# Delta net: triangular inverses as 64×64 blocks, one below the other, in place of 128×128 systems

## The chip, the cores and the metric

The kernel runs on one core of a Trainium2 chip. The metric is the time of one execution on the device in microseconds (us). PE is the matrix engine and PEld its weight loads, DVE the vector engine, ACT the scalar engine, POOL GpSimd; SP issues most DMAs. An fp32 matmul of the program appears in the trace as two passes, each with a weight load of its own.

## The reference

The program is two blocks on 256 tokens: a hybrid mixer with a mixture of experts, and a second block of four layers (forgetting attention, gated linear attention, delta net, forgetting attention). The change is in the delta-net layer, which has 8 value heads and 4 chunks of 64 tokens:

```python
def gdn_mixer(xn, w_in, conv_w, a_log, dt_bias, o_gain, w_out):
    bsz, s, _ = xn.shape
    hq, hv, d, L = GDN_QK_HEADS, GDN_V_HEADS, GDN_HEAD_DIM, GDN_CHUNK
    ...
    qkv = jax.nn.silu(causal_conv(qkv, conv_w))
    ...
    decay = jnp.where(causal, jnp.exp(jnp.where(causal, diff, 0.0)), 0.0)
    kb = kc * bc[..., None]
    vb = vc * bc[..., None]
    tri = jnp.where(strict, jnp.einsum('bhnld,bhnmd->bhnlm', kb, kc) * decay, 0.0) + jnp.eye(L, dtype=f32)
    u = lax.linalg.triangular_solve(tri, vb, left_side=True, lower=True)
    w = lax.linalg.triangular_solve(tri, kb * jnp.exp(gc)[..., None], left_side=True, lower=True)
    ...
    def step(state, inp):
        uu, ww, qkk, qd, kd, dec = inp
        v_new = uu - jnp.einsum('bhld,bhdv->bhlv', ww, state)
        o = jnp.einsum('bhld,bhdv->bhlv', qd, state) + jnp.einsum('bhlm,bhmv->bhlv', qkk, v_new)
        state = state * dec[..., None, None] + jnp.einsum('bhld,bhlv->bhdv', kd, v_new)
        return state, o
    ...
    return (o * jax.nn.silu(z)) @ w_out
```

For each head and chunk a unit lower triangular system of size 64 (`tri`) is solved.

## The kernel before

`gdn` (L1445) first projects the layer's input, convolves q and k and builds, per head, `U`: the strictly triangular products with their decay, for two halves of 128 tokens. So there are 16 systems of 128×128 (8 heads × 2 halves), each with two triangular blocks of 64 on its diagonal; the part between the two blocks is handled later.

The inverses are built by doubling. `TV` holds T (the inverse) and V (its transpose), 16 matrices of 128×128 each. `first` (L1566) makes the inverses of the 2×2 blocks: an identity from POOL, one predicated copy on DVE (L1571), four transpositions on PE (L1563) and a copy on ACT (L1574). Then come five levels, in which blocks of 2, 4, 8, 16 and 32 are joined in pairs. The systems are worked on in four groups of four, and a level of one group is three steps:

- `lower` (L1586): four matmuls with U as weights (L1592) into one PSUM bank, a memset on POOL (L1597), and a multiplication on DVE with the mask `below` (L1598), which gives X.
- `update` (L1602): four matmuls of V and X (L1610) and an addition on DVE into T (L1611). On the last level it makes V directly.
- `flipped` (L1613): four transpositions of T (L1563) and a copy on ACT into V (L1616), not on the last level.

The loop at L1631 runs these steps staggered: `lower` of step i, `update` of step i−2, `flipped` of step i−3. Between them it places the convolutions of v (`v_dense`, whose DVE work are L346, L354 and L359), their turning (`v_turn`, L1628 and L1629) and the multiplications of the queries (L1522, L1523). The projections that feed the convolutions (L271) stand before the stage in the order of PE, in both kernels. Then `upper`, `across`, `lower_half` and `rest` (L1655 to L1684) apply the inverses to v half by half, `result` follows, and `project` multiplies with the output weights.

Each engine executes its instructions in the program's order; the tile framework places the waits, and its scheduler may move instructions of independent pieces against one another when the program is built. PSUM tiles come from two pools of four banks (`ps`, `pd`). The constants `below` and `above` are made in `second_consts` (L1035 to L1050) on POOL.

## Time and profile before

| | us |
|---|---|
| median of 3 runs (lowest, highest) | 1313.79 (1312.56, 1315.02) |
| the profiled execution | 1312.93 |
| span of its instructions | 1311.3 |
| PE busy | 1149.3 |
| DVE busy | 589.4 |
| ACT busy | 492.8 |
| POOL busy | 141.6 |

The span is the time from the first to the last instruction; the profiled execution is 1.6 us longer than its span. A busy share is an average over stages with different limits, so a stage is read by its own stretch: the length of the stretch, the busy time of every engine in it, and the clock granted to PE (1.00 is 2.4 GHz). Matmuls are pipelined: the time from one to the next is read from starts or from a chain (length over count), not from the duration of one.

### The profile page before, as it was taken

How to read it: one execution, taken by the hardware profiler on the slowest of the kernel's cores; microseconds unless marked ns; L12 is line 12 of the kernel's file. 1: busy time of each engine (PE TensorE's matmuls, PEld its weight loads, DVE VectorE, ACT ScalarE, POOL GpSimd, SP SyncE). 2: the span in 40 equal slices, each digit the busy share in tenths (PEclk: the TensorE clock that was granted, in tenths of full speed). 3: DMA queues.
4: the chain of work that ended last, by engine and by line, in shares of the span. 5: the costliest groups of instructions: out<-in, count | busy, mean ns of one | idle time of the engine just before them, and what ended most of it. 6: DMA issues, size and time to landing. Idle time of an engine off the chain costs nothing.

```text
span 1311.3 us, 19298 instructions
## 1 busy us (share of the span) xinstructions
PE 1149.3 (88%) x7578; PEld 856.7 (65%) x7579; DVE 589.4 (45%) x1128; ACT 492.8 (38%) x1002; POOL 141.6 (11%) x420
## 2 busy tenths in 40 slices
PE   5999999987577676776767899999999999999998
PEld 4998999641223131321314788989788989897887
DVE  3976676410111010110102555666457776665554
ACT  4554455110101010100003467657455552356763
POOL 2000632000000000000000233010002111002310
PEclk8999999998889899888989999999999999999999
DMA  7843647899989999999999455444325430165620
GB/s 224 284 131 115 194 164 264 286 420 420 411 351 417 418 420 420 418 418 418 419 420 326 140 153 160 146 156 160 131 97 161 129 98 1 26 156 172 162 96 33
DMA packets 128633, 312.74 MB, mean 238 GB/s; under 512 B 7751, under 2 KB 73034, under 8 KB 112794
## 3 DMA queue, kind: packets, MB, share of 16 engines
q1 hardware_dynamic: 128186, 311.26, 65.6%
q8 instruction: 61, 1.00, 0.3%
q0 software_dynamic: 352, 0.20, 0.1%
q14 instruction: 34, 0.28, 0.1%
HBM read 310.39 MB, written 1.05 MB: 237 GB/s over the span
## 4 chain that ended last, share of the span: by engine, by line
PE 44%; DMA 22%; ACT 2%; DVE 2%; issue 1%; POOL 1%; SPq 0%; DVEq 0%; ACTq 0%
PE pd L292 19%; DMA we<-in_w_up 10%; PE pd L271 8%; DMA we<-in_w_down 7%; DMA we<-in_w_gate 4%; PE pd L959 2%; PE ps L1610 1%; PE ps L1592 1%; PE pd L980 1%; DMA w<-in_fox_w_in 1%; DVE wl L242 1%; ACT wh L241 1%; PE ps L1563 1%; PE ps L1176 1%; PE ps L991 1%
## 5 line engine op out<-in xcount | busy, mean ns | idle before, releaser
L271 PE MATMUL pd<-x,wh 128*128 128x256 f32 x1744 | 326.0, 287 | 2.3 <-DVE x L155 1.2
L242 DVE TENSOR_TENSOR wl<-w,wh 128x1024 fp32r<-128x1024 f32 (+1 forms) x206 | 251.1, 1223 | 127.3 <-ACT wh L241 126.7
L241 ACT CAST wh<-w 128x1024 fp32r<-128x1024 f32 (+1 forms) x206 | 214.5, 1045 | 205.5 <-PE pd L271 104.5
L271 PEld LDWEIGHTS pd<-x,wh 128*128 128x128 f32 x1744 | 275.2, 193 | 5.3 <-DVE x L155 1.8
L292 PE MATMUL pd<-wh,x 128*128 128x512 f32 (+3 forms) x896 | 252.7, 371 | 10.2 <-ACT wh L241 4.3
L271 PE MATMUL pd<-x,wl 128*128 128x256 f32 x872 | 248.1, 286 | 0.8 <-DVE wl L242 0.8
L959 PE MATMUL pd<-we,xt 128*32 128x512 f32 x1012 | 173.4, 724 | 79.1 <-DMA we<-in_w_up 50.6
L292 PEld LDWEIGHTS pd<-wh,x 128*128 128x128 f32 x896 | 162.1, 193 | 38.0 <-ACT wh L241 5.7
L959 PEld LDWEIGHTS pd<-we,xt 128*32 128x32 f32 x1012 | 40.0, 127 | 205.0 <-issue 86.4
L271 PEld LDWEIGHTS pd<-x,wl 128*128 128x128 f32 x872 | 167.7, 193 | 1.6 <-DVE wl L242 1.3
L292 PE MATMUL pd<-wl,x 128*128 128x512 f32 (+3 forms) x448 | 160.3, 370 | 1.5 <-DVE wl L242 1.4
L980 PE MATMUL pd<-we,sq 128*32 128x512 f32 x512 | 100.3, 642 | 33.9 <-DMA we<-in_w_down 28.1
L292 PEld LDWEIGHTS pd<-wl,x 128*128 128x128 f32 x448 | 85.2, 192 | 15.7 <-DVE wl L242 2.8
L992 DVE TENSOR_TENSOR hT<-hT,ps 128x512 f32<-128x512 f32 x32 | 22.0, 687 | 156.9 <-PE ps L991 156.9
L980 PEld LDWEIGHTS pd<-we,sq 128*32 128x32 f32 x512 | 24.7, 114 | 102.4 <-DMA we<-in_w_down 50.9
L969 DVE SCALAR_TENSOR_TENSOR cv<-cv,pd 128x512 f32<-128x512 f32 x8 | 5.5, 688 | 127.1 <-PE pd L959 127.1
L98 POOL TENSOR_SCALAR rq_y<-rs_v 128x8 int32<-128x8 int32 (+2 forms) x24 | 6.3, 264 | 514.9 <-DVE rs_v L186 417.0
L974 ACT COPY sq<-ps 128x512 f32<-128x512 f32 x8 | 4.7, 585 | 145.5 <-PE ps L972 145.5
L986 ACT COPY ys<-pd 128x512 f32<-128x512 f32 x16 | 9.4, 585 | 128.4 <-PE pd L980 128.4
L301 DVE SCALAR_TENSOR_TENSOR cv<-th,pd 128x512 f32<-128x512 f32 x8 | 5.5, 686 | 97.4 <-ACT th L300 97.4
L1299 POOL MEMSET at<- 128x1024 f32 x1 | 1.0, 952 | 438.1 <-DMA we<-in_w_down 438.1
L300 ACT ACTIVATE th<-pd 128x512 f32<-128x512 f32 x8 | 4.8, 597 | 100.7 <-PE pd L959 100.7
(476 smaller groups left out, 1407.3 us busy)
## 6 DMA issues: line engine op xcount, KB each, us to landing
we<-in_w_down SPq DMA_DIRECT2D x45, 1024.0 KB, 12.5
we<-in_w_up SPq DMA_DIRECT2D x40, 1024.0 KB, 12.4
we<-in_w_gate SPq DMA_DIRECT2D x37, 1024.0 KB, 12.4
w<-in_fox_w_in SPq DMA_DIRECT2D x30, 1024.0 KB, 8.0
we<-in_w_up SPq DMA_DIRECT2D x48, 512.0 KB, 13.8
we<-in_w_gate SPq DMA_DIRECT2D x46, 512.0 KB, 15.2
w<-in_w_in SPq DMA_DIRECT2D x22, 1024.0 KB, 9.2
we<-in_w_down SPq DMA_DIRECT2D x38, 512.0 KB, 14.9
```

Of the source, the lines that this page charges most:

```text
L241: nc.scalar.copy(h, v[:, k:k + m])
L242: nc.vector.tensor_tensor(l, v[:, k:k + m], h, OP.subtract)
L271: nc.tensor.matmul(acc[:, c], w[k][:, cs], x[:, k, p], start=start and c == 0 and at == 0 and i == 0, stop=stop and at == KC - 1 and i == ...
L292: nc.tensor.matmul(acc[j], x[:, k, p, ts], w[k], start=k == order[0] and i == 0 and (n != T or j == 0), stop=k == order[-1] and i == 2, sk ...
L959: mm = nc.tensor.matmul(out[32 * j:32 * j + 32], xt[:, k, 32 * j:32 * j + 32], w[name, 4 * q + j, k // 4][k % 4], start=k == 0, stop=k == ...
L980: mm = nc.tensor.matmul(py[h][32 * j:32 * j + 32], at[:, f, 32 * j:32 * j + 32], w["w_down", 4 * q + j, f // 2][f % 2][:, 512 * h:512 * h ...
L991: nc.tensor.matmul(pt[:, i * T:(i + 1) * T], ys[c // 4][:, c % 4 * P:(c % 4 + 1) * P], gst, start=True, stop=True)
L992: nc.vector.tensor_tensor(hT[:, 2 * u:2 * u + 2], hT[:, 2 * u:2 * u + 2], pt.rearrange("p (i t) -> p i t", i=2), OP.add)
L1176: nc.tensor.transpose(pt[:, (2 * i + j) * P:(2 * i + j + 1) * P], n4[w, j][:, 2 * o + i], s.ident)
L1563: nc.tensor.transpose(pt[:, a * P:(a + 1) * P], x[:, a], s.ident)
L1592: nc.tensor.matmul(pt[:, a * P:(a + 1) * P], U[:, 2 * g4 + a // 2, (a % 2) * P:(a % 2 + 1) * P], t[:, a], start=True, stop=True)
L1610: nc.tensor.matmul(pt[:, a * P:(a + 1) * P], l[:, a], m[:, a], start=True, stop=True)
```

## The change

A system is now a 64×64 block. The two blocks of a half stand one below the other: block 0 in partitions 0 to 63, block 1 in partitions 64 to 127, so TV is [128, 2, 16, 64]. Each product is one matmul per block on a quarter of the PE array (rows and columns 0 to 63, or 64 to 127), with both blocks' results in the same PSUM bank on different partitions (`products`). There are two groups of eight in place of four groups of four. V is no longer a transposition of T: `update` forms two products, one for T and one for V, into one bank, and adds both on DVE; `flip`, `flipped` and the copies of L1616 are gone. `lower` and `update` move only the 32 columns that are used. The loop goes level by level: `lower` of both groups, a `v_dense`, `update` of both, a `v_turn`; the queries come in levels 2 and 3. The masks are remade per half with 14 small copies on POOL, `upper` works in two row halves, and `lower_half` reads the 64×64 block.

```diff
+    below = s.tmp.tile([P, 5, 32], F32, tag="kk", name="below", bufs=1)
+    nc.gpsimd.memset(below, 1.0)
...
+    s.below = s.const.tile([P, 5, 16], F32, name="below")
+    s.above = s.const.tile([P, 32], F32, name="above")
+    s.ident64 = s.const.tile([P, 64], F32, name="ident64")
+    for o in range(2):
+        rows = slice(64 * o, 64 * o + 64)
+        for i in range(5):
+            n = 16 >> i
+            nc.gpsimd.tensor_copy(s.below[rows, i, :n], below[rows, i, n * o:n * o + n])
+        nc.gpsimd.tensor_copy(s.above[rows], above[rows, 32 * o:32 * o + 32])
+        nc.gpsimd.tensor_copy(s.ident64[rows], s.ident[rows, rows])
...
-        return s.conv_silu(None, pq, rb2, lambda i, j: cw[:, 16 * j + 2 * u + i:16 * j + 2 * u + i + 1], after=made.get(2))
+        return s.conv_silu(None, pq, rb2, lambda i, j: cw[:, 16 * j + 2 * u + i:16 * j + 2 * u + i + 1], after=made.get(1))
...
-    TV = s.xp.tile([P, 2, 16, P], F32, tag="x", name="TV")
+    TV = s.xp.tile([P, 2, 16, 64], F32, tag="x", name="TV")
...
-    def flip(x):
-        pt = s.ps.tile([P, 512], F32, name="ps")
-        for a in range(4):
-            nc.tensor.transpose(pt[:, a * P:(a + 1) * P], x[:, a], s.ident)
-        return pt.rearrange("p (a t) -> p a t", a=4)
-
-    def first(g4):
-
-        t, v = sys4(Tm, g4), sys4(Vm, g4)
-        nc.gpsimd.tensor_copy(v, s.ident[:, None, :].to_broadcast([P, 4, P]))
-        odd = lambda x: x.rearrange("p o (n c) -> p o n c", c=2)[:, :, :, 1]
-        made[g4] = nc.vector.copy_predicated(odd(v.rearrange("p (o j) t -> p o (j t)", o=2)).rearrange("p o (j n) -> p o j n", j=2),
-                                  s.above.bitcast(I32)[:, None, None, :].to_broadcast([P, 2, 2, P // 2]),
-                                  odd(U[:, 2 * g4:2 * g4 + 2, :T]).rearrange("p o (j n) -> p o j n", j=2)).ins
-        nc.scalar.copy(t, flip(v))
...
+    both = [(slice(64 * o, 64 * o + 64), 64 * o) for o in range(2)]
+
+    def eight(t, g):
+        return t[:, 8 * g:8 * g + 8]
 
     def halves(x, lev):
 
         x = x.rearrange("p a (n c) -> p a n c", c=4 << lev)
         return x[:, :, :, :2 << lev], x[:, :, :, 2 << lev:]
 
-    def lower(i):
-
-        lev, g4 = divmod(i, 4)
-        t = sys4(Tm, g4)
-        pt = s.ps.tile([P, 512], F32, name="ps")
-        for a in range(4):
-            nc.tensor.matmul(pt[:, a * P:(a + 1) * P], U[:, 2 * g4 + a // 2, (a % 2) * P:(a % 2 + 1) * P], t[:, a],
-                             start=True, stop=True)
-        X[i] = s.tmp.tile([P, 4, P], F32, tag="kq"[i % 2], name="X")
-        xl, xr = halves(X[i], lev)
+    def products(out, l, m):
+
+        for a in range(8):
+            for rows, off in both:
+                nc.tensor.matmul(out[rows, a], l(a, rows, off), m(a, rows), start=True, stop=True)
+
+    def bank():
+        return s.ps.tile([P, 512], F32, name="ps")
+
+    def first(g):
+
+        t, v = eight(Tm, g), eight(Vm, g)
+        nc.gpsimd.tensor_copy(v, s.ident64[:, None, :].to_broadcast([P, 8, 64]))
+        for rows, off in both:
+            made[g] = nc.vector.copy_predicated(
+                v[rows].rearrange("p (o j) (n c) -> p o j n c", j=2, c=2)[:, :, :, :, 1],
+                s.above[rows].bitcast(I32)[:, None, None, :].to_broadcast([64, 4, 2, 32]),
+                U[rows, 4 * g:4 * g + 4, :T].rearrange("p o (j n c) -> p o j n c", j=2, c=2)[:, :, :, off // 2:off // 2 + 32, 1]).ins
+        pt = bank().rearrange("p (a t) -> p a t", a=8)
+        products(pt, lambda a, rows, off: v[rows, a], lambda a, rows: s.ident64[rows])
+        nc.scalar.copy(t, pt)
...
-    def lower(i):
-
-        lev, g4 = divmod(i, 4)
-        t = sys4(Tm, g4)
-        pt = s.ps.tile([P, 512], F32, name="ps")
-        for a in range(4):
-            nc.tensor.matmul(pt[:, a * P:(a + 1) * P], U[:, 2 * g4 + a // 2, (a % 2) * P:(a % 2 + 1) * P], t[:, a],
-                             start=True, stop=True)
-        X[i] = s.tmp.tile([P, 4, P], F32, tag="kq"[i % 2], name="X")
-        xl, xr = halves(X[i], lev)
+    def products(out, l, m):
+
+        for a in range(8):
+            for rows, off in both:
+                nc.tensor.matmul(out[rows, a], l(a, rows, off), m(a, rows), start=True, stop=True)
+
+    def bank():
+        return s.ps.tile([P, 512], F32, name="ps")
+
+    def first(g):
+
+        t, v = eight(Tm, g), eight(Vm, g)
+        nc.gpsimd.tensor_copy(v, s.ident64[:, None, :].to_broadcast([P, 8, 64]))
+        for rows, off in both:
+            made[g] = nc.vector.copy_predicated(
+                v[rows].rearrange("p (o j) (n c) -> p o j n c", j=2, c=2)[:, :, :, :, 1],
+                s.above[rows].bitcast(I32)[:, None, None, :].to_broadcast([64, 4, 2, 32]),
+                U[rows, 4 * g:4 * g + 4, :T].rearrange("p o (j n c) -> p o j n c", j=2, c=2)[:, :, :, off // 2:off // 2 + 32, 1]).ins
+        pt = bank().rearrange("p (a t) -> p a t", a=8)
+        products(pt, lambda a, rows, off: v[rows, a], lambda a, rows: s.ident64[rows])
+        nc.scalar.copy(t, pt)
+
+    for g in range(2):
+        first(g)
+
+    X, last = {}, [None]
+
+    def lower(lev, g):
+
+        nb = 16 >> lev
+        tl = halves(eight(Tm, g), lev)[0]
+        pt = bank()[:, :T].rearrange("p (a t) -> p a t", a=8)
+        products(pt, lambda a, rows, off: U[rows, 4 * g + a // 2, (a % 2) * P + off:(a % 2) * P + off + 64],
+                 lambda a, rows: tl[rows, a])
+        X[g] = s.tmp.tile([P, 8, 64], F32, tag="kq"[g], name="X")
+        xl, xr = halves(X[g], lev)
         nc.gpsimd.memset(xr, 0.0)
-        nb = P // (4 << lev)
-        last[0] = nc.vector.tensor_tensor(
-            xl, halves(pt.rearrange("p (a t) -> p a t", a=4), lev)[0],
-                                s.below[:, lev, :nb][:, None, :, None].to_broadcast([P, 4, nb, 2 << lev]), OP.mult).ins
-
-    def update(i):
-
-        lev, g4 = divmod(i, 4)
-        t, v, x = sys4(Tm, g4), sys4(Vm, g4), X[i]
-        l, m, out, side = (v, x, t, 0) if lev < 4 else (x, v, v, 1)
-        out = halves(out, lev)[side]
-        pt = s.ps.tile([P, 512], F32, name="ps")
-        for a in range(4):
-            nc.tensor.matmul(pt[:, a * P:(a + 1) * P], l[:, a], m[:, a], start=True, stop=True)
-        nc.vector.tensor_tensor(out, out, halves(pt.rearrange("p (a t) -> p a t", a=4), lev)[side], OP.add)
-
-    def flipped(i):
-        lev, g4 = divmod(i, 4)
-        if lev < 4:
-            nc.scalar.copy(halves(sys4(Vm, g4), lev)[1], halves(flip(sys4(Tm, g4)), lev)[1])
+        last[0] = nc.vector.tensor_tensor(xl, pt.rearrange("p a (n c) -> p a n c", n=nb),
+                                          s.below[:, lev, :nb][:, None, :, None].to_broadcast([P, 8, nb, 2 << lev]), OP.mult).ins
+
+    def update(lev, g):
+
+        nb = 16 >> lev
+        t, v, x = eight(Tm, g), eight(Vm, g), X[g]
+        pt = bank().rearrange("p (i a t) -> p i a t", i=2, a=8)
+        xl, vr = halves(x, lev)[0], halves(v, lev)[1]
+        for i in range(lev == 4, 2):
+            if i == 0:
+                products(pt[:, 0], lambda a, rows, off: v[rows, a], lambda a, rows: xl[rows, a])
+            else:
+                products(pt[:, 1], lambda a, rows, off: x[rows, a], lambda a, rows: vr[rows, a])
+        for i, y in enumerate((t, v)):
+            if i or lev < 4:
+                out = halves(y, lev)[i]
+                nc.vector.tensor_tensor(out, out, pt[:, i].rearrange("p a (n c) -> p a n c", n=nb), OP.add)
...
-    for i in range(20 + 3):
-        if i < 20:
-            lower(i)
-        if 0 <= i - 2 < 20:
-            update(i - 2)
-        if 0 <= i - 3 < 20:
-            flipped(i - 3)
-        if i % 5 == 0 and i < 20:
-            v_dense(i // 5)
-        if i % 5 == 4 and i < 20:
-            v_turn(i // 5)
-        if i >= 10 and i < 10 + 8 and i % 2 == 0:
+    for lev in range(5):
+        for g in range(2):
+            lower(lev, g)
+        if lev < 4:
+            v_dense(lev)
+        for g in range(2):
+            update(lev, g)
+        if lev < 4:
+            v_turn(lev)
+        if lev in (2, 3):
             with s.tc.issue_after(last[0]):
-                queries((i - 10) // 2)
+                queries(2 * lev - 4)
+                queries(2 * lev - 3)
...
-            nc.tensor.matmul(pa[:, o * P:(o + 1) * P], Vm[:, 2 * h + j], v[:, j, h * P:(h + 1) * P],
-                             start=o == 0, stop=False, skip_group_check=True)
+            for rows in (lo, hi):
+                nc.tensor.matmul(pa[rows, o * P:(o + 1) * P], Vm[rows, 2 * h + j], v[rows, j, h * P:(h + 1) * P],
+                                 start=o == 0, stop=False, skip_group_check=True)
...
-            nc.tensor.matmul(pa[hi, o * P:(o + 1) * P], Vm[hi, 2 * h + j, hi], nb[hi, o * P:(o + 1) * P],
+            nc.tensor.matmul(pa[hi, o * P:(o + 1) * P], Vm[hi, 2 * h + j], nb[hi, o * P:(o + 1) * P],
```

How the order of the instructions differs, at the places around the inversions:

On PE, the start of the inversions in the program before: `ident,TV` are transpositions of V into T, `TV,U` is `lower`, `X,TV` is `update`, `ident,cv` the turning of v.

```order
2651 L1563 MATMUL ps<-ident,TV 128x128 x16
2652 L1592 MATMUL ps<-TV,U 128x128 x12
2653 L1610 MATMUL ps<-X,TV 128x128 x4
2654 L1592 MATMUL ps<-TV,U 128x128 x4
2655 L1610 MATMUL ps<-X,TV 128x128 x4
2656 L1563 MATMUL ps<-ident,TV 128x128 x4
2657 L1592 MATMUL ps<-TV,U 128x128 x4
2658 L1610 MATMUL ps<-X,TV 128x128 x4
2659 L1563 MATMUL ps<-ident,TV 128x128 x4
2660 L1628 MATMUL ps<-ident,cv 128x128 x4
```

On PE, the same place in the program after; all the products now have the line of the helper, so they are told apart by their operands: `ident,TV` is `first`, `TV,U` is `lower`, `X,TV` and `TV,X` are the two products of `update`, sixteen matmuls each.

```order
2647 L1583 MATMUL ps<-ident_1261,TV 64x64 x17
2648 L1583 MATMUL ps<-TV,U 64x32 x15
2649 L1583 MATMUL ps<-ident_1261,TV 64x64 x15
2650 L1583 MATMUL ps<-TV,U 64x32 x17
2651 L1583 MATMUL ps<-X,TV 64x32 x16
2652 L1583 MATMUL ps<-TV,X 64x32 x16
2653 L1583 MATMUL ps<-X,TV 64x32 x16
2654 L1583 MATMUL ps<-TV,X 64x32 x16
2655 L1645 MATMUL ps<-ident,cv 128x128 x4
2656 L1583 MATMUL ps<-TV,U 64x32 x32
```

Before, two `lower` stand between the `lower` of a group and its `update`, for which three other groups supply the work; after, both groups' `lower` of a level stand together, then both groups' `update`.

On DVE, the same stretch before: `cv` and `pad` belong to the convolutions of v, `X` is the masking in `lower`, `TV<-TV,ps` the addition in `update`.

```order
652 L354 SCALAR_TENSOR_TENSOR cv<-pad,gconv_half,cv 128x256 x5
653 L1598 TENSOR_TENSOR X<-ps,below 128x128x2
654 L346 TENSOR_TENSOR pad<-pd,rstd_b 128x2x256
655 L1598 TENSOR_TENSOR X<-ps,below 128x128x2
656 L359 SCALAR_TENSOR_TENSOR cv<-th,cv 128x512
657 L1598 TENSOR_TENSOR X<-ps,below 128x128x2
658 L354 SCALAR_TENSOR_TENSOR cv<-pad,gconv_half,cv 128x256 x2
659 L1611 TENSOR_TENSOR TV<-TV,ps 128x128x2
660 L354 SCALAR_TENSOR_TENSOR cv<-pad,gconv_half,cv 128x256 x2
661 L1598 TENSOR_TENSOR X<-ps,below 128x128x2
```

And after, with the same names.

```order
652 L1616 TENSOR_TENSOR X<-ps,below 128x128x2
653 L346 TENSOR_TENSOR pad<-pd,rstd_b 128x2x256
654 L359 SCALAR_TENSOR_TENSOR cv<-th,cv 128x512
655 L354 SCALAR_TENSOR_TENSOR cv<-pad,gconv_half,cv 128x256 x5
656 L1616 TENSOR_TENSOR X<-ps,below 128x128x2
657 L354 SCALAR_TENSOR_TENSOR cv<-pad,gconv_half,cv 128x256
658 L346 TENSOR_TENSOR pad<-pd,rstd_b 128x2x256
659 L359 SCALAR_TENSOR_TENSOR cv<-th,cv 128x512
660 L1633 TENSOR_TENSOR TV<-TV,ps 128x128x2 x4
661 L354 SCALAR_TENSOR_TENSOR cv<-pad,gconv_half,cv 128x256 x5
```

Before, one to five rows of the convolution stand between two rows of the inversion; after, seven instructions of the convolution stand between the X of group 0 and the X of group 1, and the four additions of a level stand in one row.


## Rows read from the trace of the kernel before

**Rows 1.** The page: the span, the busy time of each engine, and the chain that ended last by engine.

```profile
span 1311.3 us, 19298 instructions
PE 1149.3 (88%) x7578; PEld 856.7 (65%) x7579; DVE 589.4 (45%) x1128; ACT 492.8 (38%) x1002; POOL 141.6 (11%) x420
PE 44%; DMA 22%; ACT 2%; DVE 2%; issue 1%; POOL 1%; SPq 0%; DVEq 0%; ACTq 0%
```

**Rows 2.** Stretches of the delta-net layer and of what follows it. The columns are the stretch, its length, busy time and count of PE, PEld, DVE, ACT and POOL, the granted clock, the share of the DMA engines and GB/s.

```profile
1071.30:1117.30 46.00, 46.00 (x413) 45.88 (x414) 32.77 (x88) 13.91 (x31) 4.98 (x16) 1.00 0.00 1
1117.30:1140.40 23.10, 23.10 (x194) 20.84 (x194) 13.02 (x46) 8.01 (x27) 0.00 (x0) 1.00 0.01 2
...
1144.00:1169.00 25.00, 24.02 (x199) 23.82 (x200) 19.71 (x40) 14.39 (x23) 0.00 (x0) 1.00 0.61 147
1169.00:1311.30 142.30, 136.46 (x740) 115.88 (x738) 77.15 (x138) 83.68 (x193) 28.08 (x74) 0.99 0.43 122
```

**Rows 3.** The chain of waits through the start of the stage: start, length, what it went through.

```profile
1070.46 0.65 DVE TV L1571
1071.11 0.14 issue
1071.25 0.63 PE ps L1563 x4
1071.87 2.68 PE ps L1592 x24
1074.55 0.89 PE ps L1610 x8
1075.45 0.89 PE ps L1592 x8
```

**Rows 4.** Groups of instructions from 1067 to 1118 us, shapes kept apart: line, engine, operation, output and inputs, shapes, count, then busy time in us, mean ns of one, and idle time before them with what ended it.

```profile
L1592 PE MATMUL ps<-TV,U 128*128 128x128 f32 x160 | 20.8, 275 | 0.0
L354 DVE SCALAR_TENSOR_TENSOR cv<-pad,gconv_half,cv 128x256 f32<-128x256 f32 x24 | 10.5, 478 | 0.1
L1598 DVE TENSOR_TENSOR X<-ps,below 128x256 f32<-128x256 f32 x20 | 8.4, 422 | 9.2 <-PE ps L1592 8.8 <-issue 0.4
L1611 DVE TENSOR_TENSOR TV<-TV,ps 128x256 f32<-128x256 f32 x20 | 8.3, 416 | 3.6 <-PE ps L1610 3.6
L1616 ACT COPY TV<-ps 128x256 f32<-128x256 f32 x16 | 6.1, 380 | 25.4 <-PE ps L1563 25.4
L1522 DVE TENSOR_TENSOR Qd<-Qd,qkp 128x256 f32<-128x256 f32 x8 | 3.3, 415 | 0.0
L346 DVE TENSOR_TENSOR pad<-pd,rstd_b 128x512 f32<-128x512 f32 x4 | 2.8, 690 | 0.0
L359 DVE SCALAR_TENSOR_TENSOR cv<-th,cv 128x512 f32<-128x512 f32 x4 | 2.7, 682 | 0.0
L1523 DVE TENSOR_TENSOR Qx<-Qx,qkp 128x128 f32<-128x128 f32 x8 | 2.3, 284 | 0.0
L1571 DVE COPY_PREDICATED TV<-above,U 128x256 f32<-128x256 int32 x2 | 1.4, 724 | 0.0
L1628 PE MATMUL ps<-ident,cv 128*128 128x128 f32 x16 | 2.4, 272 | 0.0
```

**Rows 5.** Durations of the weight loads of L1592 and L1682 over the whole execution: smallest, median and largest in ns, then the first and the last start in us.

```profile
L1592 PEld LDWEIGHTS ps<-TV,U x160: 190/192/192, 1071.6 to 1112.8; 128*128 128x128 f32 x160
L1682 PEld LDWEIGHTS pd<-nb,TV x32: 129/133/133, 1118.8 to 1132.0; 64*64 64x64 f32 x32
```

**Rows 6.** The timeline where L1672 (rows 0 to 63 of the array) and L1682 (rows 64 to 127) meet: start, length, instruction.

```profile
1118.83 0.13 PEld L1672 LDWEIGHTS ps<-v,U 64*64 64x64 f32 x1
1118.84 0.13 PEld L1682 LDWEIGHTS pd<-nb,TV 64*64 64x64 f32 x1
1118.88 0.13 PEld L1672 LDWEIGHTS ps<-v,U 64*64 64x64 f32 x1
1118.90 0.13 PEld L1682 LDWEIGHTS pd<-nb,TV 64*64 64x64 f32 x1
1119.10 0.27 PE L1672 MATMUL ps<-v,U 64*64 64x128 f32 x1
1119.11 0.27 PE L1682 MATMUL pd<-nb,TV 64*64 64x128 f32 x1
1119.21 0.27 PE L1672 MATMUL ps<-v,U 64*64 64x128 f32 x1
1119.22 0.27 PE L1682 MATMUL pd<-nb,TV 64*64 64x128 f32 x1
```

**Rows 7.** The chain through sixteen passes with a full weight load and one moving column.

```profile
1023.71 1.68 PE ps L1493 x16
```

**Rows 8.** A stretch of an earlier layer in which PE waits, in the columns of rows 2.

```profile
1004.00:1008.00 4.00, 2.72 (x7) 2.20 (x8) 4.00 (x8) 2.48 (x4) 0.00 (x0) 0.71 0.01 4
```

**Rows 9.** The timeline of POOL where the constants are made: start, length, instruction, idle time before it.

```profile
150.85 0.30 POOL L1028 COPY btri<-tri 128x128 f32<-128x128 f32 x1
...
172.28 0.20 POOL L98 TENSOR_SCALAR rq_y<-rs_v 128x8 int32<-128x8 int32 x1 [5.70 <-DVE rs_v L186]
```

**Rows 10.** From the groups of PE in the stretch 1071.3 to 1117.3, in the columns of rows 4: `upper`, as far as it stands in that stretch.

```profile
L1664 PE MATMUL pd<-v,TV 128*128 128x128 f32 x8 | 1.2, 275 | 0.0
```

**Rows 11.** The timeline of PEld at a change from 64 columns to 128, in the columns of rows 9.

```profile
1117.74 0.97 PEld L1664 LDWEIGHTS pd<-v,TV 128*128 128x128 f32 x8 [0.17 <-DVE v L1666]
```

More of the change, by code (lines that the diff above doesn't have):

```diff
@@ L1036, in second_consts @@
                             base=0, channel_multiplier=-1)
-    s.below = s.const.tile([P, 5, 32], F32, name="below")
-    nc.gpsimd.memset(s.below, 1.0)
+    below = s.tmp.tile([P, 5, 32], F32, tag="kk", name="below", bufs=1)
+    nc.gpsimd.memset(below, 1.0)
     for i in range(5):
         b = 2 << i
-        v = s.below[:, i, :P // (2 * b)]
+        v = below[:, i, :P // (2 * b)]
         na = P // (2 * b)
@@ L1045, in second_consts @@
         nc.gpsimd.affine_select(v, v, pattern=[[2 * b, na]], compare_op=OP.is_gt, fill=0.0, base=2 * b, channel_multiplier=-1)
-    s.above = s.const.tile([P, P // 2], F32, name="above")
-    nc.gpsimd.memset(s.above, 0.0)
-    nc.gpsimd.affine_select(s.above, s.above, pattern=[[-2, P // 2]], compare_op=OP.not_equal, fill=1.0, base=0,
+    above = s.tmp.tile([P, P // 2], F32, tag="qkp", name="above", bufs=1)
+    nc.gpsimd.memset(above, 0.0)
+    nc.gpsimd.affine_select(above, above, pattern=[[-2, P // 2]], compare_op=OP.not_equal, fill=1.0, base=0,
                             channel_multiplier=1)
+    s.below = s.const.tile([P, 5, 16], F32, name="below")
[8 more added lines that the diff above has]
+        nc.gpsimd.tensor_copy(s.ident64[rows], s.ident[rows, rows])
     s.gdn_b = s.const.tile([P, 2, 8], F32, name="gdn_b")
@@ L1554, in gdn @@
     systems(1, kn, qn)
-    def sys4(t, g4):
-        return t[:, 4 * g4:4 * g4 + 4]
-    def flip(x):
-        pt = s.ps.tile([P, 512], F32, name="ps")
-        for a in range(4):
-            nc.tensor.transpose(pt[:, a * P:(a + 1) * P], x[:, a], s.ident)
-        return pt.rearrange("p (a t) -> p a t", a=4)
-    def first(g4):
-        t, v = sys4(Tm, g4), sys4(Vm, g4)
-        nc.gpsimd.tensor_copy(v, s.ident[:, None, :].to_broadcast([P, 4, P]))
-        odd = lambda x: x.rearrange("p o (n c) -> p o n c", c=2)[:, :, :, 1]
-        made[g4] = nc.vector.copy_predicated(odd(v.rearrange("p (o j) t -> p o (j t)", o=2)).rearrange("p o (j n) -> p o j n", j=2),
-                                  s.above.bitcast(I32)[:, None, None, :].to_broadcast([P, 2, 2, P // 2]),
-                                  odd(U[:, 2 * g4:2 * g4 + 2, :T]).rearrange("p o (j n) -> p o j n", j=2)).ins
-        nc.scalar.copy(t, flip(v))
-    for g4 in range(4):
-        first(g4)
-    X, last = {}, [None]
+    both = [(slice(64 * o, 64 * o + 64), 64 * o) for o in range(2)]
+    def eight(t, g):
+        return t[:, 8 * g:8 * g + 8]
     def halves(x, lev):
```

## The prediction

> **What bounds the kernel now.** I began with the page: PE is busy for 88% of the span, and 44% of the chain that ended last is PE, 22% DMA [rows 1]. That is an average, so I went to the stretch that the change rewrites. From 1071.3 to 1117.3 us PE is busy for all 46.0 us at a granted clock of 1.00, DVE for 32.8, ACT for 13.9, and the DMA engines move nothing [rows 2]. The chain of waits through it is an unbroken series of L1592, L1610 and L1563 [rows 3]: eight passes take 0.89 us, so 111 ns each. PE bounds the stage; DVE waits 8.8 us for L1592 and 3.6 us for L1610 [rows 4]. Behind the stage PE stays at 23.1 of 23.1, 24.0 of 25.0 and 136.5 of 142.3 us [rows 2]. So what the stage wins or loses reaches the end of the program almost undiminished, and I carry it over whole.
>
> **PE, what goes.** L1592, L1610 and the transpositions after `first` are 160 + 160 + 64 passes, and `first` has another 16: 400 × 0.111 = 44.4 us. With 16 passes of v_turn (1.8 us) that is the stage.
>
> **PE, what comes.** `first` 32 matmuls, five `lower` 160, four double `update` and a single one 288: 480 matmuls, 960 passes, 480 on each half of the rows. The question is the time from one pass to the next. No row of before shows a 64×64 product with 32 moving columns, so I bound it.
> - The load. A weight load takes 192 ns with 128 columns and 133 with 64 [rows 5]: 59 ns for 64 columns. Two loads of one row half follow each other after 50 to 60 ns (1118.83 and 1118.88, 1118.84 and 1118.90) [rows 6]. So 55 ns.
> - The moving. 128 columns go by in 0.11 us (1119.10, 1119.21) [rows 6], so 32 in about 27 ns.
> - Whether one hides the other. Sixteen passes with a full load and one moving column take 1.68 us, 105 ns each [rows 7]; with 128 moving columns it is 111 ns [rows 3]. The moving hides the load or the load the moving; the longer one counts, here 55 ns.
> - Whether the two row halves run side by side. L1672 in rows 0 to 63 and L1682 in rows 64 to 127 start loads 10 ns apart and each keeps its 0.11 us [rows 6]: both at once. So one pass costs 55 / 2 = 28 ns, seen over both halves.
> The low end is 20 ns, if a load of 64 rows by 64 columns is quicker than the gaps between two that may have waited for their data; the high end is 55 ns, if the halves alternate. I take 28, since the rows 6 show just this pair of quarters of the array. 960 × 28 = 26.9 us, with v_turn 28.7: 17 us less than before.
>
> **DVE.** It loses ten maskings (0.42) and two additions (0.42), 5.0 us, since both groups hold twice as many systems of half the size and the shapes stay 128×256 [rows 4]. Its four predicated copies on 64 partitions keep 256 elements, so I leave them at 0.72. From the first copy, at about 1069.8 (the last of two ends at 1071.11 before, each 0.65 [rows 3]), to the last addition it has: copies 1.45 of the four that fall in the stage, pads 2.8, L354 24 × 0.44 = 10.6, L359 2.7, ten X 4.2, eighteen additions 7.6, queries 3.3 + 2.3: 34.9 us. DVE could not end before 1104.7.
>
> **The hand-overs.** Now PE has 28.7 us and DVE 34.9 us of work in the same place, and neither is full; the order decides. A level is: `lower` of both groups (1.8 us of PE), X on DVE, `update` of both (3.6), additions, the next `lower`. The rows of the order show seven instructions of the convolution between X of group 0 and X of group 1 of level 0, so the second `update` waits 3 to 4 us there, while PE has only 1.8 us of `update` of group 0 to fill it. And the first addition of a group waits for all 32 matmuls of its `update`. I laid the new order of the three engines out with these durations, each instruction starting when its engine is free and its inputs are there, 0.35 us from a last pass to its reader and 0.10 between other engines. DVE then idles 0.7 us before the first convolution, 1.9 in all in level 1 and before level 2 (0.4, 0.1, 1.4), 0.9 and 0.8 around level 2, 0.7 in level 3 and 1.8 in level 4, with 0.1 elsewhere: 6.9 us. 1104.7 + 6.9 = 1111.6, against 1117.3: **5.7 us earlier**. In the same layout 20 ns a pass gives 1109.3, 35 gives 1114.7, 41 gives 1118.0 and 55 gives 1127.4.
>
> **The rest.** ACT loses sixteen copies of 0.38 us [rows 4], which nothing waited for for long; costed at nothing, the cover being the PE passes between. Behind the stage `upper` now comes whole after the last inverse, where before eight of its passes already lay inside [rows 10]: + 0.9 us. Its two row halves side by side cost what the full array did. Changes of layout cost 0.17 us each [rows 11], and the blocks of sixteen and eight matmuls in the new order have about two fewer of them: −0.3. Sum +0.6, with bounds −1 and +3 (if `across` waits for the last copy of a half). The 14 small copies of constants cost at most 14 × 0.30 = 4.2 us on POOL, the price of a 128×128 copy; 5.7 us of idle POOL lie behind them [rows 9]. They may push the chain of small POOL operations in between, so 0 to +1; I take 0. Other instructions of the earlier layers changed places by a few rows: ±1, taken as 0.
>
> **Sum.** −5.7 + 0.6 = −5.1 on the profiled execution of 1312.93, so 1307.8. The median of the runs is 0.9 above it; against that it is 1308.7. I write **1308.5**.
>
> **The rivals.**
> - *The halves do not run side by side.* Both now write the same PSUM bank, in different partitions; in rows 6 the pair had two banks (`ps` and `pd`). If the second waits for the first, a pass costs 55 ns, PE has 52.8 + 1.8 us and is the bound again; the layout gives +10.1, with the rest +0.6: **1324.5**. It decides from about 40 ns a pass on. For it: no row shows two row halves in one bank. Against it: the rows 6 pair is slowed by nothing, and the partitions are apart. The Trainium skill, "TensorEngine Tiling (Array Packing)", section Restrictions and Gotchas, says that different row tiles cannot access the same PSUM bank simultaneously and leaves the synchronization to software; no run here shows it so far, and by it this rival would hold. 12%.
> - *Load and moving add up within a half.* 55 + 27 = 82 ns, 41 over both halves: stage +0.7, sum +1.3, **1315**. For it: with both so short, fixed parts may show; against it: rows 7. 10%.
> - *The hand-overs are dearer.* With 0.2 us more in each of them the layout ends at 1114.0 to 1114.8: **1311.5**. For it: every level now has four hand-overs with little else on PE. 14%, half of it faster by more than the bound.
> - *PE is quicker than I think,* 20 ns or fewer waits because the scheduler's order fits better: 1104.7 to 1109.3, **1304**. 8%.
> - *The clock falls.* PE now idles about 13 of 42 us in short pieces. After a stretch in which PE waited much the granted clock was 0.71 [rows 8]; over the whole stage that would make 28 ns into 39 and the time about **1314**; if it stayed at the lower level, 1.2 GHz, 56 ns and 1324. Against it: the stretches around the stage, small gaps included, all show 0.99 or 1.00 [rows 2]. 4%.
>
> **How the numbers follow.** The forecast (24 to 32 ns, 1305 to 1311) has 52%. Within 0.2%, which is 2.6 us and about what a measurement can tell here, means 1311.2 to 1316.4. Faster: 52 + 8 + half of the dear hand-overs is near 0.63. Same: the other half and most of the 41 ns case, 0.17. Slower: the halves in turn, the clock and what is left, 0.20. The range 1303 to 1320 leaves out the first rival, the slow clock and a little below.
>
> **What would show it.** In the stretch after the first predicated copy: sixteen matmuls of `lower`, 32 passes, in 0.9 us (right), 1.3 (load and moving add up) or 1.8 (halves in turn). Starts of rows 0 to 63 and 64 to 127 about 10 ns apart against 55. DVE busy for five sixths of the stage, with PE waiting for X of group 1 in levels 0 to 2. Granted clock 1.00. The last addition near 1111.6, and the stretch from there to the end of `rest` and `result` about 23.7 long. I am wrong if PE is without a gap through the stage, or if the time moved before 1060 us.

## The result and the profile after

The changed kernel takes 1328.76 us (median of 4 runs, 1327.87 to 1330.03), the kernel before beside it 1314.09 (4 runs, 1312.56 to 1315.02): ratio 1.0123, 95% interval 1.0104 to 1.0141. It is slower by 15 us; 1308.5 was forecast. The profiled execution took 1330.03 us. A ratio, here and below, is estimated from all runs of the two kernels; it is not the quotient of the two medians.

The head of the page of the changed kernel, with busy times and the granted clock in forty slices, against [rows 1]:

```profile
span 1328.5 us, 20396 instructions
PE 1157.4 (87%) x8170; PEld 862.9 (65%) x8171; DVE 585.9 (44%) x1116; ACT 485.8 (37%) x984; POOL 139.8 (11%) x422
PEclk7999999998879888988989999999999975899999
```

DVE does 3.5 us less, ACT 7.0 and POOL 1.8 (5.0 and 6.1 were counted for DVE and ACT); PE is busy for longer although its passes are smaller. The clock row shows a dip at 7, 5, 8 near the end. Stretches of the changed kernel around it, in the columns of [rows 2]:

```profile
1071.30:1082.50 11.20, 8.47 (x153) 6.77 (x151) 9.51 (x22) 6.56 (x19) 0.56 (x2) 1.00 0.34 75
1082.50:1137.00 54.50, 54.46 (x891) 52.55 (x891) 27.98 (x72) 7.62 (x16) 1.87 (x6) 0.50 0.01 2
1137.00:1160.00 23.00, 22.12 (x208) 20.54 (x207) 14.74 (x48) 9.21 (x30) 0.00 (x0) 0.99 0.01 2
```

From 1082.5 to 1137 us the granted clock is 0.50, the 1.2 GHz level, and PE is busy for 54.46 of 54.50 us. The timeline of PE in the changed kernel (start, length, instruction, idle time before it):

```profile
1080.57 1.12 PE L1583 MATMUL ps<-TV,U 64*64 64x32 f32 x32 [0.79 <-ACT TV L1599]
1082.54 1.88 PE L1583 MATMUL ps<-X,TV 64*64 64x32 f32 x32 [0.85 <-DVE X L1616]
1084.22 1.91 PE L1583 MATMUL ps<-TV,X 64*64 64x32 f32 x32
...
1094.31 1.92 PE L1583 MATMUL ps<-X,TV 64*64 64x32 f32 x32
1096.04 1.90 PE L1583 MATMUL ps<-TV,X 64*64 64x32 f32 x32
```

The last `lower` of level 0 is 32 passes in 1.12 us with the tail of the last one. From 1082.54 on, the next such block starts about 1.7 us later (1082.54 to 1084.22, 1094.31 to 1096.04): 53 to 54 ns a pass in place of 28. DVE now waits for PE where PE was to wait for DVE; the groups of the changed kernel from 1060 to 1140 us:

```profile
L1633 DVE TENSOR_TENSOR TV<-TV,ps 128x256 f32<-128x256 f32 x18 | 6.8, 417 | 13.6 <-PE ps L1583 13.6
L1616 DVE TENSOR_TENSOR X<-ps,below 128x256 f32<-128x256 f32 x10 | 4.2, 420 | 7.0 <-PE ps L1583 7.0
```

The counts, 18 additions and 10 maskings, and their 0.42 us are those of the forecast. That is one loss. The other lies ahead of the stage. One instruction just before the inversions, the masking of the last products, in the timeline of DVE before and after:

```profile
1068.04 0.54 DVE L1537 TENSOR_TENSOR kk<-ps,strict 128x384 f32<-128x384 f32 x1
```

```profile
1074.59 0.56 DVE L1548 TENSOR_TENSOR kk<-ps,strict 128x384 f32<-128x384 f32 x1
```

It comes 6.6 us late. The last addition of the inversions started at 1116.89 and now starts at 1132.44, 15.6 late; the span is 17.2 longer. So 6.6 us are lost before the stage, 9.0 in it and 1.7 behind it, in this one pair of executions. The constants are made at 150 to 173 us; POOL in the changed kernel there:

```profile
164.17 0.47 POOL L1060 COPY above<-above 64x32 f32<-64x32 f32 x2
164.72 1.13 POOL L106 TENSOR_TENSOR rq_t<-rq_t,rs_v 128x8 f32<-128x8 f32 x1
165.80 3.14 POOL L1059 COPY below<-below 64x16 f32<-64x16 f32 x10
169.03 0.20 POOL L107 TENSOR_SCALAR rq_t<-rq_t 128x8 f32<-128x8 f32 x1
...
172.54 0.21 POOL L108 TENSOR_TENSOR rstd<-rq_t,rq_y 128x8 f32<-128x8 f32 x1
```

and the end of the same chain of small operations before:

```profile
166.38 0.20 POOL L108 TENSOR_TENSOR rstd<-rq_t,rq_y 128x8 f32<-128x8 f32 x1
```

L98 to L108 compute a reciprocal square root step by step. Ten copies stand between two of its steps, two more just ahead of them, and its result comes 6.2 us later. About 1 us of that is there before the first copy: L1028 starts at 151.92, before at 150.85. DVE reads the result in L478, before and after:

```profile
167.62 0.42 DVE L478 COPY sq<-rstd 128x512 f32<-128x512 f32 x1
```

```profile
172.78 0.43 DVE L478 COPY sq<-rstd 128x512 f32<-128x512 f32 x1 [1.23 <-POOL rstd L108]
```

Before, it found the result there; now it waits for POOL and comes 5.2 us late.

### The profile page after: what moved, and what is told of

Its sections match the earlier page's. It is cut to its first block, busy times and chain, and to the rows that moved or that the text cites. A ratio compares the mean times of both kernels' runs of the same rounds, so it can differ in the third digit from the quotient of the medians.

```text
span 1328.5 us, 20396 instructions
## 1 busy us (share of the span) xinstructions
PE 1157.4 (87%) x8170; PEld 862.9 (65%) x8171; DVE 585.9 (44%) x1116; ACT 485.8 (37%) x984; POOL 139.8 (11%) x422
## 4 chain that ended last, share of the span: by engine, by line
PE 43%; DMA 23%; DVE 2%; ACT 2%; issue 1%; POOL 1%; SPq 0%; DVEq 0%; ACTq 0%
PE pd L292 19%; PE pd L271 9%; DMA we<-in_w_up 8%; DMA we<-in_w_down 8%; DMA we<-in_w_gate 6%; PE ps L1583 3%; PE pd L959 2%; PE pd L980 1%; DMA w<-in_fox_w_in 1%; DVE wl L242 1%; PE ps L1187 1%; ACT wh L241 1%; PE ps L1205 1%; PE ps L1086 0%; PE ps L1544 0%
## 5 line engine op out<-in xcount | busy, mean ns | idle before, releaser
L959 PE MATMUL pd<-we,xt 128*32 128x512 f32 x1012 | 167.5, 696 | 84.5 <-DMA we<-in_w_up 57.9
L980 PE MATMUL pd<-we,sq 128*32 128x512 f32 x512 | 106.2, 659 | 34.0 <-DMA we<-in_w_down 28.2
L292 PEld LDWEIGHTS pd<-wl,x 128*128 128x128 f32 x448 | 84.8, 191 | 15.6 <-DVE wl L242 2.8
L98 POOL TENSOR_SCALAR rq_y<-rs_v 128x8 int32<-128x8 int32 (+2 forms) x24 | 6.1, 254 | 528.4 <-DVE rs_v L186 435.4
```

Of the source, the lines that this page charges most:

```text
L98: e.tensor_scalar(y.bitcast(I32), v.bitcast(I32), -0.5, float(0x5F3759DF), op0=OP.mult, op1=OP.add)
L292: nc.tensor.matmul(acc[j], x[:, k, p, ts], w[k], start=k == order[0] and i == 0 and (n != T or j == 0), stop=k == order[-1] and i == 2, sk ...
L959: mm = nc.tensor.matmul(out[32 * j:32 * j + 32], xt[:, k, 32 * j:32 * j + 32], w[name, 4 * q + j, k // 4][k % 4], start=k == 0, stop=k == ...
L980: mm = nc.tensor.matmul(py[h][32 * j:32 * j + 32], at[:, f, 32 * j:32 * j + 32], w["w_down", 4 * q + j, f // 2][f % 2][:, 512 * h:512 * h ...
```

## The experiments

Each is compared with runs of the kernel before on the same chip. Two theories for the stage: N, the narrow passes keep the clock down; W, the waits of PE at the start bring it down. Two for the shift ahead of it: C, the copies on POOL; O, other instructions that changed places.

**The copies alone.** The kernel before, with the 14 copies behind its constants:

```diff
+    for o in range(2):
+        rows = slice(64 * o, 64 * o + 64)
+        for i in range(5):
+            n = 16 >> i
+            nc.gpsimd.tensor_copy(s.below_h[rows, i, :n], s.below[rows, i, n * o:n * o + n])
...
```

> The kernel before with the 14 small POOL copies of the change added behind its constants, their results unused; nothing else differs. Theory C (the copies stand in a chain of reciprocal square roots on POOL and delay all that follows): the instructions at 1060 us come 4 to 9 us later than in before and the time is 1318 to 1323. Rival O (the other instructions that changed places in the mixer and in the mixture of experts make the shift): within 2 us of before, 1312 to 1316.

Measured 1320.69 us against 1314.25, ratio 1.0049 (1.0032 to 1.0066): 6.4 us from copies whose results nobody reads; the masking that stood at 1068.04 stands at 1073.37, 5.3 us late. For these 6.4 us C has no rival, since the source differs in nothing else. How they pass through is seen in two stretches at 200 to 235 us. Before:

```profile
200.00:220.00 20.00, 19.54 (x162) 19.12 (x161) 13.92 (x24) 10.29 (x16) 8.73 (x25) 1.00 0.75 267
220.00:235.00 15.00, 15.00 (x131) 15.00 (x130) 7.18 (x9) 5.92 (x10) 0.00 (x0) 1.00 0.82 282
```

With the copies:

```profile
200.00:220.00 20.00, 18.10 (x148) 17.51 (x147) 12.43 (x22) 9.94 (x16) 8.65 (x26) 0.99 0.77 264
220.00:235.00 15.00, 14.19 (x99) 13.90 (x99) 7.76 (x12) 5.50 (x10) 0.00 (x0) 0.78 0.61 214
```

PE waits 1.4 us longer in the first stretch and 0.8 in the second, and its clock is 0.78 in the second, where it was 1.00: 99 passes fit where 131 did. The stretches are fixed in time and so do not hold quite the same work, but single instructions agree: L186 of DVE, at 172.02 before, is 2.5 us late, and the first L514, at 224.24 before, is 4.7 late. Here the late result on POOL cost PE twice, by the wait and by the lower clock around it.

**The copies moved in the code.** The changed kernel, with the masks of before made at the old place and the copies written at the start of `gdn`:

```diff
+    for o in range(2):
+        rows = slice(64 * o, 64 * o + 64)
+        for i in range(5):
+            n = 16 >> i
+            nc.gpsimd.tensor_copy(s.below[rows, i, :n], s.below_all[rows, i, n * o:n * o + n])
...
     zs = s.ring.tile([P, 2, D], F32, tag="w", name="zs")
```

> The changed kernel with the constants of before made at their old place and the 14 copies cut from them only at the start of the delta net, where POOL idles. Theory C: the start of the inversions lies within 2 us of where it would be without any shift (first predicated copy near 1069 to 1071, 1076.9 in the changed kernel) and the time falls by 6 to 9 us to about 1320 to 1323; the half clock in the stage stays. Rival O: 1327 to 1330 as the changed kernel.

Measured 1326.62, ratio 1.0104 (1.0082 to 1.0125). Twelve of the copies had not moved: the scheduler put them where they were, as POOL's timeline of this kernel shows (the two of the identity it put at 3 us, near the start of the program).

```profile
163.57 0.20 POOL L106 TENSOR_TENSOR rq_t<-rq_t,rs_v 128x8 f32<-128x8 f32 x1
163.72 3.15 POOL L1461 COPY below<-below_all 64x16 f32<-64x16 f32 x10
166.95 1.23 POOL L107 TENSOR_SCALAR rq_t<-rq_t 128x8 f32<-128x8 f32 x1
```

So this run does not test C as it was meant to. To hold the copies back they need an input that exists only in the delta net:

```diff
+    one = s.tmp.tile([P, 8], F32, name="ss")[:, :1]
+    nc.gpsimd.tensor_scalar(one, r[:, 0:1], 0.0, 1.0, op0=OP.mult, op1=OP.add)
...
-            nc.gpsimd.tensor_copy(s.below[rows, i, :n], below[rows, i, n * o:n * o + n])
+            nc.gpsimd.tensor_tensor(s.below[rows, i, :n], s.below_all[rows, i, n * o:n * o + n], one[rows].to_broadcast([64, n]), OP.mult)
```

> The changed kernel with its 14 constant copies held back to the delta net: each multiplies by a one that is computed on POOL from the layer's own reciprocal, so that the scheduler can't move it up. Theory C (the copies in POOL's chain delay everything): the first predicated copy comes 4 to 7 us earlier than in the changed kernel and the time is 1320 to 1324, with the half clock in the stage unchanged. Rival O (other instructions that changed places): 1327 to 1330.

Measured 1325.83 (1323.05 to 1328.08), ratio 1.0115 (1.0079 to 1.0151); the profiled execution took 1324.04. There the masking that was 6.6 us late is back, 1.0 us before its old place:

```profile
1067.02 0.56 DVE L1549 TENSOR_TENSOR kk<-ps,strict 128x384 f32<-128x384 f32 x1
```

So the copies make the shift ahead of the stage. In the profiled executions this masking is 2.3 to 6.7 us late in the eight kernels that have the copies in POOL's chain, and 0.3 to 1.0 us early in four that hold them back. Why the shift differs among the eight was not looked into, and O is not excluded as a part of it: a kernel below is 9.2 us late there with its copies held back.

The time of this version shows little of the gain: 1320 to 1324 was expected, and its ratio can't be told from the 1.0123 of the changed kernel. Part of the gain goes again at the start of the stage, where PE waits for ACT's copy of group 1 in `first` (L1600):

```profile
1074.62 0.63 ACT L357 ACTIVATE th<-cv 128x512 f32<-128x512 f32 x1 [2.14 <-DVE cv L354]
1075.16 0.57 ACT L1600 COPY TV<-ps 128x512 f32<-128x512 f32 x1
```

```profile
1075.78 1.92 PE L1584 MATMUL ps<-TV,U 64*64 64x32 f32 x32 [3.57 <-ACT TV L1600]
```

The copy now stands behind an activation of the convolution that waits for DVE; in the changed kernel it did not, and PE waited 0.79 us. From the masking to the last addition the stage takes 60.2 us here, 57.9 in the changed kernel. The half clock is still there (1074.0 to 1128.6 at 0.50).

**More moving columns.** In `lower`, T is moved with all its 64 columns, though only 32 results are used:

```diff
-        tl = halves(eight(Tm, g), lev)[0]
-        pt = bank()[:, :T].rearrange("p (a t) -> p a t", a=8)
+        tl = eight(Tm, g)
+        pt = bank().rearrange("p (a t) -> p a t", a=8)
```

> The changed kernel with 64 moving columns in lower and update in place of 32 (the two products of update in two banks); the count of passes, the waits at the start and the constants are those of the changed kernel. Theory N (the clock falls and stays down because the passes move few columns on two quarters of the array): granted clock 1.00 through most of the stage, 28 to 30 ns a pass, the stage about 12 us shorter, 1315 to 1318. Rival W (the waits of PE at the start of the stage bring the clock down): half clock as in the changed kernel, 55 ns a pass, 1327 to 1331.

As run, the edit had reached `lower` alone; `update` still moved 32 columns. Measured 1311.58 against 1314.25, ratio 0.9997 (0.9980 to 1.0013). With the two products of `update` widened too, each in a bank of its own:

```diff
-                products(pt[:, 0], lambda a, rows, off: v[rows, a], lambda a, rows: xl[rows, a])
+                products(pts[i], lambda a, rows, off: v[rows, a], lambda a, rows: x[rows, a])
...
-                products(pt[:, 1], lambda a, rows, off: x[rows, a], lambda a, rows: vr[rows, a])
+                products(pts[i], lambda a, rows, off: x[rows, a], lambda a, rows: v[rows, a])
```

> The changed kernel with 64 moving columns in lower and in both products of update (two banks in place of one); e3_wide as run had widened lower alone. Theory N (few moving columns keep the clock down) together with a load of 55 ns a pass that hides up to 64 columns: clock 1.00 over the stage or a shorter stretch of half clock than the 6.8 us of e3_wide, 28 to 30 ns a pass, 1308 to 1312. If the moving columns cost time of their own (load and moving add up): 41 ns a pass at full clock, 1317 to 1323.

Measured 1312.37 against 1313.08, ratio 1.0003 (0.9986 to 1.0020). And `update` alone widened, by the same two lines:

> The changed kernel with 64 moving columns in update alone and 32 in lower. Theory N: two thirds of the passes of the levels are wide, so the clock stays at 1.00 or falls for less time than in e3_wide (where one third was wide, 6.8 us), one time of 1309 to 1316. Rival: a stretch of half clock as long as in the changed kernel, 54.6 us, 1326 to 1331.

One time, 1311.69. The stretch of the inversions in the three kernels, with `lower` wide, all wide, and `update` wide:

```profile
1080.00:1120.00 40.00, 35.86 (x916) 34.11 (x914) 29.22 (x76) 8.30 (x18) 1.87 (x6) 0.91 0.01 3
```

```profile
1075.00:1117.00 42.00, 33.99 (x991) 31.75 (x992) 32.47 (x83) 11.01 (x24) 1.95 (x7) 1.00 0.03 7
```

```profile
1071.30:1120.00 48.70, 42.59 (x1046) 40.25 (x1045) 36.03 (x92) 12.94 (x29) 2.42 (x8) 0.89 0.03 8
```

More columns, with the same number of passes, bring 0.50 up to 0.89, 0.91 and 1.00 in these three executions. In the kernel with all passes wide, PE waits at the start as it did in the changed kernel, and longer:

```profile
1082.78 1.15 PE L1583 MATMUL ps<-X,TV 64*64 64x64 f32 x32 [0.92 <-DVE X L1616]
1083.73 1.13 PE L1583 MATMUL ps<-TV,X 64*64 64x64 f32 x32
1086.36 1.15 PE L1583 MATMUL ps<-X,TV 64*64 64x64 f32 x32 [1.50 <-DVE X L1616]
```

32 passes take 0.95 us (1082.78 to 1083.73), 30 ns each: the 64 columns cost 1 ns over what 32 cost at the full clock (29 ns, rows below). This fits a load that still hides them.

**Filling the waits.** The changed kernel with four full 128×128 matmuls behind each `lower`, results unused:

```diff
         for g in range(2):
             lower(lev, g)
+            fill()
```

> The changed kernel with four full 128x128 matmuls (eight passes, results unused) behind each of the ten lower, so that PE has wide work where it waited; the passes of lower and update keep 32 columns. Rival W: the clock stays at 1.00, the stage about 8 us shorter than in the changed kernel, 1319 to 1323. Theory N, if the narrow passes alone keep the clock down: half clock over most of the stage, eight passes cost 1.8 us each time, 5 to 18 us longer, 1334 to 1347. If wide work between narrow passes is enough to keep the clock: as rival W, and then only the two runs together tell N from W.

Measured 1345.39, ratio 1.0246 (1.0216 to 1.0276). Eight full passes behind every 32 narrow ones of `lower` did not hold the clock:

```profile
1075.00:1086.80 11.80, 9.57 (x242) 9.02 (x243) 10.24 (x23) 3.54 (x7) 0.32 (x2) 1.00 0.01 3
1086.80:1148.00 61.20, 61.20 (x806) 57.37 (x807) 21.16 (x57) 5.21 (x10) 1.56 (x5) 0.50 0.01 2
```

Not all waits were filled (1.56 us for X of group 1 remained), so this run alone doesn't settle W. The next takes other waits away: each convolution is issued only after both maskings of its level.

```diff
-        return s.conv_silu(None, pq, rb2, lambda i, j: cw[:, 16 * j + 2 * u + i:16 * j + 2 * u + i + 1], after=made.get(1))
+        return s.conv_silu(None, pq, rb2, lambda i, j: cw[:, 16 * j + 2 * u + i:16 * j + 2 * u + i + 1], after=last[0] or made.get(1))
```

> The changed kernel with 32 columns as it is, and each convolution issued on DVE after the masking of both groups, which takes away PE's waits of 0.85 us for X at the start of the stage. Theory N (the narrow passes bring the clock down): half clock over most of the stage all the same, one time of 1324 to 1333. Rival W (those waits bring it down): clock 1.00 in the first levels, 1313 to 1320.

One time, 1326.62. Both `update` of the first level run through without a wait; then PE waits for the convolution, and the clock is down:

```profile
1080.61 1.10 PE L1583 MATMUL ps<-X,TV 64*64 64x32 f32 x32
1081.55 1.10 PE L1583 MATMUL ps<-TV,X 64*64 64x32 f32 x32
1082.48 1.10 PE L1583 MATMUL ps<-X,TV 64*64 64x32 f32 x32
1083.41 1.10 PE L1583 MATMUL ps<-TV,X 64*64 64x32 f32 x32
1086.33 1.12 PE L1645 MATMUL ps<-ident,cv 128*128 128x128 f32 x4 [1.82 <-DVE cv L359]
1087.38 3.63 PE L1583 MATMUL ps<-TV,U 64*64 64x32 f32 x64
```

A wait had only changed its place, so W isn't ruled out as what lets the clock fall. But from 1087.4 to 1136 us PE waits 0.9 us in all, and the granted clock is 0.53: as what keeps the clock down W is out. These rows also give the plain price of a narrow pass at 1.00: 0.93 us for 32, 29 ns, with both row halves in one bank.

**Both mends**, by the edits above. `lower` alone widened, copies held back:

> lower with 64 moving columns, update with 32, and the 14 copies held back to the delta net as in f1_held. If the two causes (clock and copies) are independent, the time is that of e3_wide less what f1_held gains: 1304 to 1308. If the copies' delay was hidden anyway: 1310 to 1313.

Measured 1311.93 against 1313.08, ratio 1.0001 (0.9986 to 1.0017): no better than with the copies in their chain. Its granted clock over the inversions was lower than with the copies in place, 0.81 from 1074 to 1110 us, where it had been 0.91 from 1080 to 1120. The second and third row are the stretch of PE's wait for ACT, which this version has too, and what follows it:

```profile
1074.00:1110.00 36.00, 31.09 (x771) 29.64 (x773) 26.13 (x69) 7.64 (x15) 1.87 (x6) 0.81 0.01 3
1073.00:1076.50 3.50, 0.00 (x1) 0.00 (x0) 3.46 (x8) 1.37 (x4) 0.00 (x0) 0.79 0.00 0
1076.50:1088.00 11.50, 11.47 (x196) 11.07 (x198) 6.59 (x17) 2.81 (x6) 0.62 (x2) 0.50 0.01 1
```

```profile
1076.53 1.97 PE L1584 MATMUL ps<-TV,U 64*64 64x64 f32 x32 [3.53 <-ACT TV L1600]
```

The clock falls within this wait and is back at 1.00 by 1089 us, when PE is in the 64 wide passes of the next `lower`.

With all passes wide:

> Both mends together: 64 moving columns in lower and update as in e6_allwide, and the 14 copies held back to the delta net as in f1_held. If copies and clock are independent: clock 1.00 through the inversions, no shift before them, 1304 to 1308 and faster than before by more than 0.2%. If the early shift was mostly taken back later: 1309 to 1313.

Measured 1306.11 against 1311.99, 12 runs against 16, ratio 0.9960 (0.9948 to 0.9972). This version beats both kernels. Its stretch through the inversions, and the part of it in which PE waits:

```profile
1068.00:1108.00 40.00, 31.28 (x926) 29.33 (x927) 30.96 (x80) 10.66 (x24) 1.87 (x6) 1.00 0.02 6
1072.60:1076.10 3.50, 0.02 (x1) 0.00 (x0) 3.46 (x8) 1.36 (x4) 0.00 (x0) 1.00 0.00 0
```

and the wait itself:

```profile
1076.16 1.15 PE L1584 MATMUL ps<-TV,U 64*64 64x64 f32 x32 [3.54 <-ACT TV L1600]
```

A wait of 3.54 us, and the clock stays at 1.00. This can't be put down to the wide passes alone: in the version with `lower` alone widened, PE had run the same passes up to the same wait (`first` and `lower` of group 0, all with 64 columns; 3.53 us), and there the clock fell. The profiled execution is also the fastest of the twelve (1304.62); for the others no trace shows the stage.

**Two that failed.** The making of the masks moved as well, by the same `one`:

```diff
-    nc.gpsimd.memset(s.below_all, 1.0)
+    nc.gpsimd.tensor_copy(s.below_all, one[:, :, None].to_broadcast([P, 5, 32]))
...
-    nc.gpsimd.memset(s.above_all, 0.0)
+    nc.gpsimd.tensor_tensor(s.above_all, one.to_broadcast([P, P // 2]), one.to_broadcast([P, P // 2]), OP.subtract)
```

> As f2_wide_held, and the making of both masks (two fills and eleven selections on POOL, 4.9 us in before between 151 and 163 us) stands in the delta net too. Theory C says that this takes more from the same chain: 3 to 6 us below f2_wide_held, 1299 to 1304. Rival: the same POOL work now stands before the reciprocals of the delta net and delays those: not below f2_wide_held, 1305 to 1312.

Measured 1319.35, ratio 1.0062 (1.0037 to 1.0086). Neither reason held. The reciprocal that was to gain ended 2.6 us earlier than before (163.75 against 166.38), and the delay does not come from the delta net. It is there by 245 us:

```profile
200.00:220.00 20.00, 17.34 (x109) 17.14 (x108) 8.44 (x14) 6.54 (x10) 6.20 (x22) 0.74 0.41 142
```

The clock is 0.74 and the DMA engines move 142 GB/s where they moved 267. The scheduler had changed the places of other instructions there; which of them made PE wait was not tried.

The convolutions behind both maskings (the line of `conv_silu` above), on top of the version that beats both:

> As f5_allwide_held, and each convolution of v is issued on DVE only after the masking of both groups of its level, so that no convolution stands between the X of group 0 and the X of group 1. If the hand-overs cost what PE waited in e6_allwide for X (1.5 us in level 0, 1.6 in levels 1 and 2): 2 to 4 us below f5_allwide_held. If the convolutions now stand before the additions instead: within 2 us of it, or longer.

Measured 1318.47, ratio 1.0058 (1.0037 to 1.0078). PE no longer waits for X; it waits for the turning of v, which stands in front of the next `lower` (waits of PE from 1066 to 1150 us, sum, times, longest), and the clock falls now and then (0.84 over the stage):

```profile
PE ps L1645 <- DVE cv L359: 12.3, 4, 4.1
```

## Why the prediction was wrong

**The step that failed first** is the clock. The sum priced every pass of the stage at the full clock; "The clock falls" was given 4%, on the ground that the stretches around the stage show 0.99 or 1.00. In those stretches all but 14 of some 1,550 passes move 128 columns or more; nothing in them speaks for quarter passes with 32. The price in the rival's worst case, 1.2 GHz over the whole stage and 56 ns a pass, is what came: 54 ns, 0.50 for 54.5 us. I had priced the rival right and judged its chance by the wrong rows. Its reason was only half right: it let PE's idle pieces bring the clock down, and while the clock stayed down PE had none. Both signs of being wrong that the forecast named are there: PE without a gap through the stage, and time that moved before 1060 us.

Of the 17.2 us between the two spans, 9.0 lie in the stage, where the sum had −5.7 (its layout for 55 ns a pass had +10.1); 6.6 ahead of it, where the sum had nothing; and 1.7 behind it, where the sum had +0.6.

What lets the clock fall and what keeps it down are not the same thing. Kept down it is, in these kernels, by the narrow passes: with PE busy 54.46 of 54.50 us it did not rise, and with `lower`, `update` or both widened the stage had 0.81 to 1.00. What lets it fall first stays open. In the kernels where it fell PE had waited shortly before, 0.8 to 4.1 us, but a wait does not decide it: after the same wide passes, the same wait of 3.5 us went with a fall in one version and with none in another.

**The second step** is "they may push the chain of small POOL operations in between, so 0 to +1; I take 0". The price of the copies was right (0.47 and 3.14 us in the rows above, 0.54 for the two of the identity at 152.8: 4.15, where at most 4.2 was estimated). The cover was not: the 5.7 us of idle POOL in [rows 9] lie after the chain's result, so they can't hide what stands in front of it. They are a wait for L186 of DVE, which comes after L478 has read that result. What could absorb a delay is the slack of the reader, and L478 started 1.0 us after the result was there. The copies alone cost 6.4 us.

**Where the clock holds,** the forecast comes close, in part by luck. With all passes wide and the copies held back the same masking stands at 1067.41 and the last addition at 1109.75: 42.3 us, against 48.9 before. The stage is 6.5 shorter; 5.7 was forecast. 29 to 30 ns a pass were measured for the 28 of the sum. The median of the whole version is 5.9 us lower (the ratio gives 3.7 to 6.8); the sum said 5.1. But from the first predicated copy to the end of the last addition DVE was busy for 31.0 us and idle for 9.4, where the layout had 34.9 and 6.9. The durations had been added up, and instructions that follow each other on DVE overlap in the trace (L1522 at 1106.99 for 0.42 us, L1523 already at 1107.32); that error and the hand-overs that were too short cancel in part. So the estimate came out for a kernel that is not the changed one.

**The halves in turn** did not occur: 29 ns at 1.00 with both halves in one bank is 58 ns in each half, what [rows 6] give for the load of one half alone, so they run side by side. The Trainium skill, "TensorEngine Tiling (Array Packing)", section Restrictions and Gotchas, would not have two row tiles in one bank at once; here, on different partitions of it, no time was lost. **Load and moving** do not add up: 64 columns cost 30 ns, 32 cost 29. **The hand-overs** were dearer than laid out, as above, and the run that removed the waits for X found another wait behind them.

**The 0.63 for faster** rested on one price for PE and let every other term hang on its clock. Its parts, 52, 8 and half of 14, make 0.67.

## What to carry to other kernels

A pass that is smaller must also be judged by what it does to the clock: look at the granted clock of stretches with the same shape of pass, and where the trace has none, give the lower level a real chance. Columns that the weight load hides anyway are cheap, and here they paid for themselves. One trace in which the clock holds is not yet a rule: the same passes and the same wait went both ways here.

An idle stretch behind a chain on an in-order engine does not cover what is put in front of the chain's result; the slack that counts is that of the result's reader. And code that is moved in the source may be moved back by the scheduler, so its place is read from the trace.
